# First attention of a two-layer encoder: where its next weights are requested and split, on which queue layer 1's memory stores go, and where the rest of layer 1's bias is laid out

## The chip, the cores and the metric

One core of a Trainium2 chip. The metric is the device time of one execution in microseconds. Before the change it is 2130.92 us, the median of three runs (2130.47 to 2131.5); one more execution was taken by the profiler, and the views below are of that one.

In the profile, PE is TensorE's matmul and PEld its weight load, DVE is VectorE, ACT ScalarE, POOL GpSimd; SPq and ACTq are the queues on which SyncE and ScalarE issue DMAs, each in order.

## The reference

An encoder of two layers on 1024 tokens of width 1024, with 256 fixed memory tokens. Each layer has a token mixer, a cross attention to the memory and a SwiGLU:

```python
mem_n = rmsnorm(mem, norm_mem)
for i in range(DEPTH):                       # DEPTH = 2
    h = rmsnorm(x, norm_mix[i])
    mkv = mem_n @ w_mem_kv[i]                # memory keys and values, 4 heads
    if i % 2 == 0:
        proj = h @ w_in_a[li]                # q (12 heads), k, v (4 heads), q_mem
        y_tok = windowed_gqa(...)            # window of +-128 tokens, ALiBi, sink
    else:
        proj = h @ w_in_b[li]                # q, k, v (12 heads each), q_mem
        y_tok = neighbourhood_attn(..., rpb_b[li])   # learned 2-D bias
    y_mem = memory_attn(qm, mk, mv)
    x = x + jnp.concatenate([y_tok, y_mem], axis=-1) @ w_out[i]
    h = rmsnorm(x, norm_ffn[i])
    gu = h @ w_gate_up[i]
    x = x + (jax.nn.silu(gu[..., :D_FF]) * gu[..., D_FF:]) @ w_down[i]
return rmsnorm(x, norm_final)
```

All of it is float32. The kernel reaches that precision by writing each operand of the dense products as a high part (rounded to fp32r by a cast, `hi`) and a low part (what the cast lost, `lo`, one subtraction), and by three matmuls for each product (`three`): high by high, high by low, low by high.

## The kernel before

Activations lie transposed, 128 features on the partitions and 512 tokens in a tile; the sequence is two halves of 512, f = 0 and 1. `steps` (L131 to L144) multiplies one unit of weights, 128 output features by 1024 inputs, with one half: eight steps of three matmuls of 128x128 by 128x512, so 24 matmuls for a unit and a half. The matmuls are recorded at L140, the splits at L106 (`hi`, ACT) and L109 (`lo`, DVE, or POOL where `load_w` is told so).

The program is written in Python and traced; a planner then lays the instructions out on each engine and each DMA queue. Its starting order is that of the program, but an instruction whose inputs its model finds ready can be put ahead of an earlier one that waits. On the chip each engine and each queue keeps the order that it was given. A tile with a tag has a fixed number of buffers (`bufs`); a new tile of that tag waits for the release of an old one.

**The opening (L325 to L345).** The first weights (`raws[0]`, in two halves) and the norm vectors (`gains`, L327) are loaded on ACT's queue; x, the memory, the memory's weights (`load_wm`) on SP's. `unscaled(k)` (L352) scales tile k of x's first half by the norm vector and splits it into `hT[0][k]`; the norm's factor itself is multiplied in later. Squares for the norms are recorded at L366. The first three units of layer 0 (`FIRST`: queries and keys of head group 0, memory queries, values) are multiplied with half 0 into three sums.

**The memory's units (the loop over i from 0 to 7).** Eight units of memory weights, four for each layer. Iteration i requests unit i+4 (`load_wm`), splits unit i+2 (`split_wm`) and multiplies unit i (`mem_dense`, L425). The other steps are threaded through it: the norm of half 1, the split of half 1 into `hT[1]` (`f1`), and `finish_wm(j)`, which turns the sums of unit j into memory keys (high and low) or values (transposed on TensorE, L448, then scaled and split, L453 and L454). When a layer's keys or values are complete, they are stored to DRAM: keys at L441 (`memk_d`), values at L458 (`memv_d`), both layers on SP's queue.

**The late sums.** After the loop, the same three units are multiplied with half 1 into `late`: the first two as a pair, step by step, with what is left of `finish_wm` between their steps; then the third. Their weights are the three buffers of the tag "whl" (`wf`).

**The attention of layer 0.** Twelve units in all: `Unit.request` asks for the raw weights on SP's queue (tile `w_early`, L587), `fetch` splits them, `open` makes the tiles, `half(f)` multiplies, `put` copies a sum into queries, keys or the transposed values, `close` copies the keys to the other 64 partitions (L647) or transposes the values (`put_v`, L564). `first_units` requests units 3 to 5, puts the six sums of the first three units, and closes them. Next, in program order, are sixteen DMAs (L871) that lay layer 1's bias out in DRAM; layer 1's attention reads it.

The attention itself runs over 32 halves of heads (`Half`): `scores` (L714, softmax on DVE, ACT and POOL), `turn` (transposes of the probabilities, L757) and `mix` (L777). Between their steps `pull()` draws one step of the remaining nine units (`other_units`), at a rate such that each unit is done when its head is due: the steps left over, divided by the halves left until then.

The lines ahead of the change that matter most here:

```python
pair_steps = zip(*(steps(late[n], wf[n], hT[1]) for n in range(2)), strict=True)
for i, _ in enumerate(pair_steps):
    if i > 0:
        run_some(todo, 1)
    if i == 1:
        run(todo)
        todo = (None for j in range(4, 8) for _ in finish_wm(j))
```

Of the kernel before, what the change touches and what calls it, by code (L numbers as in the profile page):

```python
# [41 lines left out]
def trunk_kernel(ctx: ExitStack, tc: tile.TileContext, a: dict, out: bass.AP):  # L42
# [103 lines left out]
    def run(g):  # L146
        for _ in g:
            pass

    def run_some(g, n):  # L150
        for _ in range(n):
            next(g, None)
# [134 lines left out]
    with tc.tile_pool(name="mp", bufs=1, reuse_waits="tile") as mp:  # L287
# [35 lines left out]
        raws = [raw_tile("wf_raw") for _ in range(3)]  # L323
        src = [a["w_in_a"][u] for u in FIRST[0]]
        nc.scalar.dma_start(raws[0][:, :HS], src[0][:, :HS])  # L325
        load_x(0, 0, each=True)
        nc.scalar.dma_start(gains, a["gains"])  # L327
        load_x(0, 2)
# [32 lines left out]
        def total(norm, parts, n=D):  # L361
# [14 lines left out]
            yield  # L376

        split_raw(wf[0], raws[0], cs=slice(0, HS))
        for k in range(4):
            unscaled(k)  # L380
# [49 lines left out]
        def finish_wm(i):  # L430
# [4 lines left out]
            if u < 2:  # L435
                nc.vector.tensor_tensor(t, ps, scale, op=ALU.mult)
                hi(kh[:, u], t)
                lo(kl[:, u], t, kh[:, u])
                if u == 1:
                    for j, h in enumerate((kh, kl)):  # L440
                        nc.sync.dma_start(memk_d[l, j], h.rearrange("p m k -> p (m k)").bitcast(F32))  # L441
                yield
                return
# [13 lines left out]
            if u == 3:  # L457
                nc.sync.dma_start(memv_d[l], vm.rearrange("p b m i d -> p (b m i d)").bitcast(F32))  # L458
            yield

        todo, f1 = iter(()), iter(())
        for i in range(8):
# [31 lines left out]
            if i > 4:  # L494
                run_some(f1, 2)
                run_some(todo, 2)
        run(f1)
        late = [ps_mm.tile([P, HS], F32, tag="mm", name="mm") for _ in range(2)]
        pair_steps = zip(*(steps(late[n], wf[n], hT[1]) for n in range(2)), strict=True)
        for i, _ in enumerate(pair_steps):  # L500
            if i > 0:
                run_some(todo, 1)
            if i == 1:
                run(todo)
                todo = (None for j in range(4, 8) for _ in finish_wm(j))
        run(todo)
        late.append(ps_t.tile([P, HS], F32, tag="T", name="mm"))
# [3 lines left out]
    for layer in range(2):  # L511
        is_a = layer == 0
        with tc.tile_pool(name=f"ap{layer}", bufs=1, reuse_waits="tile") as ap:
# [321 lines left out]
            def first_units():  # L835
                if is_a:
                    for z in units[n0 : 2 * n0]:
                        z.request()
                for z, (z.w, *ps) in zip(units, pre):
                    z.open()  # L840
                    z.put(0, ps[0])
                for n, z in enumerate(units[:n0]):
                    if is_a:
                        z.put(1, pre[n][2])
                    else:
                        yield from z.half(1)
                    units[n0 + n].fetch()
                    z.close()

# [17 lines left out]
            at = [0]  # L867
            run(first_units())
            if is_a:
                for r in range(ROWS):  # L870
                    nc.sync.dma_start(  # L871
                        bias_d[:, r * SC : (r + 1) * SC, :],
                        a["rpb"][:, :, (ROWS - 1 - r) * 24 : (ROWS - 1 - r) * 24 + 3 * P],
                    )
            work = other_units()
# [37 lines left out]

            run(halves[0].scores())
            groups = 13
            for i in range(len(halves)):
# [9 lines left out]
                if i == 0:  # L926
                    for _ in range(8):
                        pull()
                jobs = []
                if i + 1 < len(halves):  # L930
# [755 lines left out]
```

## Time and profile before

| what | value |
|---|---|
| median of three runs | 2130.92 us (2130.47 to 2131.5) |
| the profiled execution | 2130.05 us |
| its span, which all windows and times below count from | 2128.3 us |
| TensorE busy | 2096.2 us, 98% of the span |
| VectorE, ScalarE, GpSimd busy | 71%, 50%, 27% |
| mean granted TensorE clock | 0.996 of full speed |
| TensorE busy from 71.84 to 83.08 us | 8.12 of 11.24 us, granted clock 0.70 |
| TensorE busy from 90 to 320 us (most of the first attention) | 224.97 of 230 us, granted clock 1.00 |

How to read the rows. A row of waits names the engine, the line that waited, and whose end released it, then the total in us, the number of times and the longest. A row of the timeline has the start, the time, the engine and line, the operation, the tiles written and read, and in brackets the idle time just ahead of it and its releaser. A row of windows has the stretch, its length, the busy time of the engines asked for (instructions in brackets; PE, PEld, DVE, ACT, POOL where all are shown, PE alone where there is one), the granted clock, the share of the DMA engines and GB/s. A row of the chain has start, time and what the end waited for. Ends of matmuls are modelled, so single durations overlap; a rate is taken from the chain or from a long run of them.

### The profile page before, as it was taken

Reading aid. Unit: us, or ns where it says so; the run is one execution under the profiler, and the core shown is the slowest. Engines: PE = TensorE matmul, PEld = TensorE weight load, DVE = VectorE, ACT = ScalarE, POOL = GpSimd, SP = SyncE. Lnnn points to the kernel's source line nnn. Section 1 sums busy time; section 2 is a strip of 40 time slices with the busy share of each in tenths; the row PEclk is TensorE's granted clock in tenths of the full one; section 3 lists DMA queues with packets and bytes.
Section 4 is the critical chain, followed back from the end, with each engine's and each line's share of the span. In section 5 each row is a group of like instructions: output and inputs, shape, how many; then the busy total and the mean of one; then the engine's idle time right before and its main releaser. Section 6 shows DMA issues by size and latency. Waiting matters only on the chain.

```text
span 2128.3 us, 29044 instructions
## 1 busy us (share of the span) xinstructions
PE 2096.2 (98%) x10316; PEld 1751.5 (82%) x10316; DVE 1518.6 (71%) x2476; ACT 1066.0 (50%) x2035; POOL 580.9 (27%) x618
## 2 busy tenths in 40 slices
PE   9999999999999999999999999999999999999998
PEld 7788888878888888888778888888788888888886
DVE  7687787787666666867765666667986666667675
ACT  6677775444434334344465666654443434344442
POOL 0344330233444430000233233203243444400000
PEclk9999999999999999999999999999999999999999
DMA  5421028333323227856232222274232323267662
GB/s 221 141 95 51 26 90 282 99 99 114 109 102 107 99 104 252 311 209 213 75 92 84 72 58 71 83 257 158 71 113 104 109 105 106 97 251 253 204 221 90
DMA packets 120914, 287.29 MB, mean 135 GB/s; under 512 B 12224, under 2 KB 20672, under 8 KB 120768
## 3 DMA queue, kind: packets, MB, share of 16 engines
q1 hardware_dynamic: 113312, 272.68, 37.9%
q10 hardware_dynamic: 7456, 12.74, 1.6%
q8 instruction: 82, 1.34, 0.3%
q14 instruction: 64, 0.52, 0.1%
HBM read 210.40 MB, written 68.94 MB: 131 GB/s over the span
## 4 chain that ended last, share of the span: by engine, by line
PE 89%; DVE 4%; ACT 3%; DMA 1%; issue 1%; POOL 1%; SPq 0%; DVEq 0%; POOLq 0%; ACTq 0%
PE X L1051 16%; PE Y L1051 16%; PE mm L140 15%; PE X L1482 11%; PE Y L1482 8%; PE po L140 8%; PE O L777 3%; PE S L714 3%; PE pT L757 3%; PE X L1133 2%; PE Y L1133 2%; ACT p L729 1%; PE mm L425 1%; DMA wd_kept<-in_w_dn 1%; PE bc L249 0%
## 5 line engine op out<-in xcount | busy, mean ns | idle before, releaser
L1051 PE MATMUL Y<-hB,wgu 128*128 128x512 f32 x1056 | 255.5, 391 | 0.8 <-ACT c L1071 0.8
L1051 PE MATMUL X<-hB,wgu 128*128 128x512 f32 x1056 | 254.8, 391 | 0.0
L1482 PE MATMUL X<-hB,wd 128*128 128x512 f32 (+1 forms) x1092 | 243.7, 383 | 0.9 <-DVE x L1446 0.9
L109 DVE TENSOR_TENSOR wgu<-wS,wgu 128x1024 fp32r<-128x1024 f32 (+1 forms) x124 | 152.9, 1233 | 121.7 <-ACT wgu L106 121.5
L1482 PEld LDWEIGHTS X<-hB,wd 128*128 128x128 f32 x1092 | 200.2, 188 | 41.8 <-issue 2.3
L1051 PEld LDWEIGHTS Y<-hB,wgu 128*128 128x128 f32 x1056 | 196.7, 188 | 43.4 <-ACT c L1071 1.6
L1051 PEld LDWEIGHTS X<-hB,wgu 128*128 128x128 f32 x1056 | 195.9, 188 | 39.9
L742 POOL TENSOR_SCALAR p<-p,stat 128x384 f32<-128x384 f32 (+1 forms) x256 | 142.0, 574 | 308.8 <-DVE stat L739 214.4
L140 PE MATMUL mm<-hT,wqk 128*128 128x512 f32 x672 | 197.2, 405 | 1.5 <-DVE KL L109 1.5
L106 ACT CAST wgu<-wS 128x1024 fp32r<-128x1024 f32 (+1 forms) x124 | 114.3, 923 | 150.2 <-POOL wS L1008 124.6
L140 PE MATMUL po<-yT,wo 128*128 128x512 f32 x768 | 185.0, 394 | 0.0
L1482 PE MATMUL Y<-hB,wd 128*128 128x512 f32 x792 | 181.0, 390 | 0.1
L1482 PEld LDWEIGHTS Y<-hB,wd 128*128 128x128 f32 x792 | 148.4, 188 | 32.0 <-DVE x L1446 0.8
L234 POOL TENSOR_TENSOR nr<-nv,neg_half 128x4 f32<-128x4 f32 (+1 forms) x12 | 13.4, 1118 | 585.8 <-DVE nv L233 582.0
L140 PEld LDWEIGHTS po<-yT,wo 128*128 128x128 f32 x768 | 142.7, 188 | 29.6 <-issue 1.0
L1051 PE MATMUL X<-hT,wgu 128*128 128x512 f32 x624 | 150.2, 391 | 0.0
L106 ACT CAST hB<-b_raw 128x512 fp32r<-128x512 f32 x154 | 89.5, 618 | 116.8 <-DMA b_raw<-b_d 96.7
L1008 POOL TENSOR_TENSOR wS<-wgu_raw 128x512 f32<-128x512 f32 x44 | 61.1, 1388 | 294.5 <-DVE wgu L109 294.5
L1051 PEld LDWEIGHTS X<-hT,wgu 128*128 128x128 f32 x624 | 116.7, 188 | 26.3
L729 ACT ACTIVATE p<-p,stat 128x256 f32<-128x256 f32 (+1 forms) x192 | 112.4, 587 | 51.9 <-DVE stat L725 49.9
L109 DVE TENSOR_TENSOR pl<-pT,ph 128x384 fp32r<-128x384 f32 (+1 forms) x256 | 118.2, 492 | 19.9 <-ACT ph L106 16.9
L109 DVE TENSOR_TENSOR hB<-b_raw,hB 128x512 fp32r<-128x512 f32 x154 | 100.0, 687 | 43.3 <-ACT hB L106 42.8
(208 smaller groups left out, 4232.2 us busy)
## 6 DMA issues: line engine op xcount, KB each, us to landing
wgu_raw<-in_w_gu SPq DMA_DIRECT2D x92, 512.0 KB
wd_raw<-in_w_dn SPq DMA_DIRECT2D x70, 512.0 KB
b_raw<-b_d SPq DMA_DIRECT2D x70, 512.0 KB
b_d<-c SPq DMA_DIRECT2D x88, 256.0 KB
b_d<-t SPq DMA_DIRECT2D x66, 256.0 KB
wo_raw<-in_w_out SPq DMA_DIRECT2D x32, 512.0 KB
xr_d<-x ACTq DMA_DIRECT2D x32, 256.0 KB
xr<-xr_d SPq DMA_DIRECT2D x16, 512.0 KB
```

The lines of the kernel that those rows point to most:

```text
L106: nc.scalar.copy(dst, src)
L109: (eng or nc.vector).tensor_tensor(dst, src, h.bitcast(F32), op=ALU.subtract)
L140: nc.tensor.matmul(ps[:, :n], l, r, start=start and i == 0 and j == 0, stop=stop and i == len(order) - 1 and j == 2,)
L714: nc.tensor.matmul(s_[:, :n], Q[self.h][:, qb * P : (qb + 1) * P], k, start=j == 0, stop=j == 1)
L729: nc.scalar.activation(p[:, :n], p[:, :n], AF.Exp, bias=m1, scale=-1.0, accum_out=s1)
L742: nc.gpsimd.tensor_scalar(p[:, :n], p[:, :n], ri[:, i : i + 1], 1.0, op0=ALU.mult, op1=ALU.mult)
L757: nc.tensor.transpose(tr[:, j * P : (j + 1) * P], p[:, j * P : (j + 1) * P], ident)
L777: nc.tensor.matmul(o[:, c0 : c0 + w * P], self.value(j), t[:, s0 : s0 + w].rearrange("p j q -> p (j q)"), start=j == js[0] and t is self.p ...
L1008: sub = lambda o, p_, q_: nc.gpsimd.tensor_tensor(o, p_, q_, op=ALU.subtract)
L1051: nc.tensor.matmul(ps, l, r, start=n in (0, 1, 3, 6) and k == 0 and i == 0, stop=k == 3 and i == 2, skip_group_check=True,)
L1133: nc.tensor.matmul(bank[:, at : at + h2], l, r, start=start and k == 0 and i == 0, stop=stop and k == 1 and i == 2, skip_group_check=True,)
L1482: nc.tensor.matmul(bank[:, c], l, r, start=i in (0, 1, 3, 6) and p == 0 and n == 0, stop=p == HF - 1 and n == 2, skip_group_check=True,)
```

## The change

Five edits, all ahead of or inside the first attention.

1. The norm vectors are loaded ahead of the first weights on ACT's queue, and `unscaled(0)` stands ahead of the split of these weights.
2. The stores of layer 1's memory keys and values go on ACT's queue; layer 0's stay on SP's.
3. In iteration 5 of the memory's loop, unit 3's raw weights are requested on SP's queue (`next_raw`). The pair of late sums is taken apart: `late[0]` with all its steps, then `late[1]`; at the first step of `late[1]` unit 3's weights are split, on ACT and DVE, into the buffer that `late[0]`'s weights leave. The leftover steps of `finish_wm` stand at steps 5 to 7 of the one and from step 0 on of the other.
4. Layer 0's first units become `ready_units`: units 4 and 5 alone are requested there, and three steps are drawn (`pull`) ahead of the transposes of the values. One step is also drawn behind each of the four steps of the first scores.
5. The sixteen DMAs of layer 1's bias are issued two at a time in halves 4 to 11 of the attention.

```diff
--- before.py
+++ after.py
@@ -322,9 +322,9 @@
 
         raws = [raw_tile("wf_raw") for _ in range(3)]
         src = [a["w_in_a"][u] for u in FIRST[0]]
+        nc.scalar.dma_start(gains, a["gains"])
         nc.scalar.dma_start(raws[0][:, :HS], src[0][:, :HS])
         load_x(0, 0, each=True)
-        nc.scalar.dma_start(gains, a["gains"])
         load_x(0, 2)
         nc.scalar.dma_start(raws[0][:, HS:], src[0][:, HS:])
         load_x(0, 4)
@@ -375,8 +375,9 @@
             norm.acc = [t[:, :n]]
             yield
 
+        unscaled(0)
         split_raw(wf[0], raws[0], cs=slice(0, HS))
-        for k in range(4):
+        for k in range(1, 4):
             unscaled(k)
         split_raw(wf[0], raws[0], cs=slice(HS, D))
         for k in range(4, NK):
@@ -438,7 +439,7 @@
                 lo(kl[:, u], t, kh[:, u])
                 if u == 1:
                     for j, h in enumerate((kh, kl)):
-                        nc.sync.dma_start(memk_d[l, j], h.rearrange("p m k -> p (m k)").bitcast(F32))
+                        queues[l].dma_start(memk_d[l, j], h.rearrange("p m k -> p (m k)").bitcast(F32))
                 yield
                 return
             nc.scalar.copy(t, ps)
@@ -455,10 +456,11 @@
                     vl, src[:, b], r, vh.bitcast(F32), op0=ALU.mult, op1=ALU.subtract
                 )
             if u == 3:
-                nc.sync.dma_start(memv_d[l], vm.rearrange("p b m i d -> p (b m i d)").bitcast(F32))
+                queues[l].dma_start(memv_d[l], vm.rearrange("p b m i d -> p (b m i d)").bitcast(F32))
             yield
 
-        todo, f1 = iter(()), iter(())
+        queues = nc.sync, nc.scalar
+        todo, f1, next_raw = iter(()), iter(()), []
         for i in range(8):
             if i % 4 == 0:
                 l = i // 4
@@ -494,15 +496,22 @@
             if i > 4:
                 run_some(f1, 2)
                 run_some(todo, 2)
+            if i == 5:
+                next_raw = raw_tile("wf_raw")
+                nc.sync.dma_start(next_raw, a["w_in_a"][1])
         run(f1)
         late = [ps_mm.tile([P, HS], F32, tag="mm", name="mm") for _ in range(2)]
-        pair_steps = zip(*(steps(late[n], wf[n], hT[1]) for n in range(2)), strict=True)
-        for i, _ in enumerate(pair_steps):
-            if i > 0:
-                run_some(todo, 1)
+        for i, _ in enumerate(steps(late[0], wf[0], hT[1])):
             if i == 1:
                 run(todo)
                 todo = (None for j in range(4, 8) for _ in finish_wm(j))
+            if i > 4:
+                run_some(todo, 1)
+        next_w = wp.tile([P, 2, D], F32R, tag="whl", name="wf", bufs=3)
+        for i, _ in enumerate(steps(late[1], wf[1], hT[1])):
+            run_some(todo, 1)
+            if i == 0:
+                split_raw(next_w, next_raw)
         run(todo)
         late.append(ps_t.tile([P, HS], F32, tag="T", name="mm"))
         run(steps(late[2], wf[2], hT[1]))
@@ -833,18 +842,27 @@
             n0 = 3
 
             def first_units():
-                if is_a:
-                    for z in units[n0 : 2 * n0]:
-                        z.request()
+                for z, (z.w, ps) in zip(units, pre):
+                    z.open()
+                    z.put(0, ps)
+                for n, z in enumerate(units[:n0]):
+                    yield from z.half(1)
+                    units[n0 + n].fetch()
+                    z.close()
+
+            def ready_units():
+                units[n0].w = next_w
+                for z in units[n0 + 1 : 2 * n0]:
+                    z.request()
                 for z, (z.w, *ps) in zip(units, pre):
                     z.open()
                     z.put(0, ps[0])
                 for n, z in enumerate(units[:n0]):
-                    if is_a:
-                        z.put(1, pre[n][2])
-                    else:
-                        yield from z.half(1)
+                    z.put(1, pre[n][2])
                     units[n0 + n].fetch()
+                    if z.kind == "v":
+                        for _ in range(3):
+                            pull()
                     z.close()
 
             def other_units():
@@ -865,13 +883,15 @@
 
             done = [n0]
             at = [0]
-            run(first_units())
-            if is_a:
-                for r in range(ROWS):
-                    nc.sync.dma_start(
-                        bias_d[:, r * SC : (r + 1) * SC, :],
-                        a["rpb"][:, :, (ROWS - 1 - r) * 24 : (ROWS - 1 - r) * 24 + 3 * P],
-                    )
+            if not is_a:
+                run(first_units())
+
+            def spread_bias(r):
+                nc.sync.dma_start(
+                    bias_d[:, r * SC : (r + 1) * SC, :],
+                    a["rpb"][:, :, (ROWS - 1 - r) * 24 : (ROWS - 1 - r) * 24 + 3 * P],
+                )
+
             work = other_units()
             taken = [0]
 
@@ -911,7 +931,11 @@
                 for m in range(2):
                     yield from steps(po[m], wo[m], yT[0], pairs[-2:-1], start=False, stop=False)
 
-            run(halves[0].scores())
+            if is_a:
+                ready_units()
+            for _ in halves[0].scores():
+                if is_a:
+                    pull()
             groups = 13
             for i in range(len(halves)):
 
@@ -926,6 +950,9 @@
                 if i == 0:
                     for _ in range(8):
                         pull()
+                if is_a and 4 <= i < 4 + ROWS // 2:
+                    for r in (2 * i - 8, 2 * i - 7):
+                        spread_bias(r)
                 jobs = []
                 if i + 1 < len(halves):
                     jobs.append(halves[i + 1].scores())
```

## The prediction

> **What bounds the kernel now.** The page's table of engines and its chain come first, then the waits of the matrix engine over the whole span.
>
> ```profile
> PE 2096.2 (98%) x10316; PEld 1751.5 (82%) x10316; DVE 1518.6 (71%) x2476; ACT 1066.0 (50%) x2035; POOL 580.9 (27%) x618
> PE 89%; DVE 4%; ACT 3%; DMA 1%; issue 1%; POOL 1%; SPq 0%; DVEq 0%; POOLq 0%; ACTq 0%
> ...
> PE mm L140 <- ACT hT L355: 2.5, 1, 2.5
> PE mm L140 <- ACT wqq L106: 2.4, 1, 2.4
> ```
>
> TensorE is the bound, so only its waits can be gained. The two rows of waits are single events inside the part that the diff edits: the opening (ACT hT, 2.5 us) and the first weights of layer 0's attention (ACT wqq, 2.4 us). The timeline of TensorE and the windows by stage show the second.
>
> ```profile
> 70.78 1.07 PE L140 MATMUL mm<-hT,wf 128*128 128x512 f32 x4
> 72.53 1.09 PE L564 MATMUL vtr<-ident,vT 128*128 128x128 f32 x8 [0.68 <-ACT vT L607]
> 76.07 7.01 PE L140 MATMUL mm<-hT,wqq 128*128 128x512 f32 x17 [2.45 <-ACT wqq L106]
> 82.92 0.40 PE L714 MATMUL S<-mKH,QS 128*128 128x256 f32 x2
> ...
> 58.13 4.15 PE mm L140 x18
> 52.46 0.22 PE mvT L448 x2
> ...
> 75.40:75.60 0.20, 0.00 (x0) 0.52 0.90 369
> ...
> 82.20:82.40 0.20, 0.20 (x2) 0.92 0.65 223
> ```
>
> The last product with the first three weights ends at 70.78 + 1.07 = 71.85. Then eight transposes stand alone, then 2.45 us of nothing, then 17 matmuls in 7.01 us, though 18 took 4.15 us at 58.13 (0.231 each). The windows say why: the granted clock is at half (0.52) from 75.4 and back (0.92) at 82.2. The chain of waits and SP's timeline say why the weights were late.
>
> ```profile
> 69.72 5.22 DMA w_early<-in_w_in_a
> ...
> SPq L441 <- ACT mkh L106: 19.3, 2, 18.4
> SPq L458 <- DVE mv L454: 4.4, 1, 4.4
> ...
> 67.98 0.33 SPq L458 DMA_DIRECT2D memv_d<-mv  x1
> 68.36 0.76 SPq L871 DMA_DIRECT2D bias_d<-in_rpb  x1
> 69.72 1.40 SPq L587 DMA_DIRECT2D w_early<-in_w_in_a  x3
> ```
>
> SP's queue is in order. It stood 4.4 us on the store of layer 1's memory values (memv_d, 67.98); behind it came a piece of layer 1's bias (and dist), and only at 69.72 the weights, which took 5.22 us to land, while TensorE needed them at 71.85.
>
> **The change part by part.** *The stall.* From 71.85 to the first score at 82.92 (11.07 us) TensorE did 17 matmuls (17 x 0.231 = 3.92 us) and eight transposes (8 x 0.11 = 0.88, by the mvT row): 4.80 us of work, so **6.27 us lost** (0.68 + 2.45 of waits, the rest half clock and slow transposes). Making unit 3's weights ready beforehand and queueing three steps of its product ahead of the transposes takes this away, if nothing else is late at 71.85.
>
> *What is late next: the weights.*
>
> ```profile
> 56.30 0.34 SPq L441 DMA_DIRECT2D memk_d<-mkh  x1
> 54.55 3.36 PE L140 MATMUL mm<-hT,wf 128*128 128x512 f32 x14
> 74.97 1.04 ACT L106 CAST wqq<-w_early 128x1024 fp32r<-128x1024 f32 x1 [1.40 <-DMA w_early<-in_w_in_a]
> 19.64 1.22 DVE L109 TENSOR_TENSOR wm<-wm 128x1024 fp32r<-128x1024 f32 x1
> 60.00:70.00 10.00, 10.00 (x47) 8.19 (x47) 5.21 (x13) 5.08 (x13) 0.00 (x0) 1.00 0.46 169
> ```
>
> next_raw is requested in iteration 5, ahead in program order of both layers' memory stores. If it is put behind layer 0's keys store (issued at 56.30, where SP stood 18.4 us), it lands by 56.9 + 5.2 = 62.1, by the slow w_early row. Its split (next_w) takes wf[0]'s buffer, so it must wait for the end of late[0]: 54.55 + 24 x 0.231 + 0.2 = 60.3.
>
> The split is one cast of 1.04 on ACT and one subtraction of 1.22 on DVE: ready by about 65, seven early. Both engines are half idle from 60 to 70 (DVE 5.21, ACT 5.08 of 10 us), so it costs nothing; without that cover it would be the 2.3 us. Units 4 and 5 still come by w_early, but are needed only after 48 matmuls (11 us) more.
>
> *What is late next: the bank.* Unit 3's sum takes the bank that late[0] leaves, so the puts (the copies of late[0] into queries and keys) must be done.
>
> ```profile
> 67.20 0.37 ACT L453 ACTIVATE mv<-mvT,nr 128x128 fp32r<-128x128 f32 x1 [0.42 <-DVE mv L454]
> 67.47 0.61 ACT L106 CAST QS<-first 64x512 fp32r<-64x512 f32 x1
> ...
> 73.11 0.70 DVE L109 TENSOR_TENSOR KL<-mm,KH 64x512 fp32r<-64x512 f32 x1 [0.64 <-ACT KH L106]
> 59.52 0.68 DVE L109 TENSOR_TENSOR hT<-h,hT 128x512 fp32r<-128x512 f32 x1
> ```
>
> Today the last read of it ends at 73.81, which would cost 73.81 - 71.85 = 1.96 us. What held the puts until 67.47 is the last memory value (mv, 67.20), whose transposes stand in TensorE's order after all eight steps of the pair (48 matmuls). Now the six leftover steps stand at steps 5 to 7 of late[0] and 0 to 2 of late[1], so that transpose comes after some 33: 15 x 0.231 = 3.5 us earlier. Against that ACT gains 1.04 for next_w and three stores to issue. Net some 1.3 us earlier, and late[0] itself ends 5 us earlier, so its keys need not go behind vT. Bounds 0 to 1.96; I take 0.1, near the lower end, as three of the four movements are in its favour.
>
> *late[0] alone.* One weight per step asks for a new hT every 3 x 0.231 = 0.69 us, where the pair asked every 1.4. The last hT is ready at 60.20 (DVE, 59.52); late[0]'s eighth step would want it near 59.6. Bounds: nothing (late[1]'s first steps go into the hole) to 0.6; I take 0.3.
>
> *The stores on ACT's queue.* Three issues, and waits behind DVE:
>
> ```profile
> 1.23 0.39 ACTq L327 DMA_DIRECT2D gains<-in_gains  x1
> 61.85 0.43 DVE L109 TENSOR_TENSOR mkl<-mt,mkh 128x256 fp32r<-128x256 f32 x1 [0.15 <-ACT mkh L106]
> 66.42 0.37 ACT L453 ACTIVATE mv<-mvT,nr 128x128 fp32r<-128x128 f32 x1 [2.73 <-PE mvT L448]
> ```
>
> An issue takes 0.39 us (gains); the low keys that a store waits for take 0.43 on DVE. Queued behind each on ACT are next_w's cast, the last mv and the puts, for which TensorE waits in the end. Three times 0.4 to 0.8 us is 1.2 to 2.4; ACT stands idle 2.73 us ahead of mv at 66.42, so the cost is taken as zero; without that cover up to 2.4 on the puts, which the bank's bound holds mostly.
>
> *The opening.* gains first, and unscaled(0) ahead of the split.
>
> ```profile
> 4.39 0.62 ACT L106 CAST wf<-wf_raw 128x512 fp32r<-128x512 f32 x1 [1.62 <-DMA wf_raw<-in_w_in_a]
> 5.20 1.06 ACT L366 ACTIVATE sq<-x 128x1024 f32<-128x1024 f32 x1 [0.20 <-DMA x<-in_x]
> 8.17 1.33 ACT L355 ACTIVATE hT<-x,gains 128x512 fp32r<-128x512 f32 x2 [0.69 <-DMA x<-in_x]
> 8.93 1.42 DVE L356 SCALAR_TENSOR_TENSOR hT<-x,gains,hT 128x512 fp32r<-128x512 f32 x2 [0.61 <-ACT hT L355]
> 10.00:20.00 10.00, 10.00 (x44) 8.09 (x43) 10.00 (x15) 10.00 (x16) 0.00 (x0) 1.00 1.04 403
> ```
>
> A square (1.06) is ahead of the first hT on ACT. With hT first, TensorE starts up to 1.06 earlier, less 0.39 for weights that now queue behind gains: 0.7. But at 8.17 ACT waits for x's second transfer, and from 8.93 DVE has no gap (10.00 of 10.00 in the next window), so what TensorE wins before 8 it waits away after. Bounds: -0.4 (the weights' delay shown) to +0.7; I take 0.
>
> *Bias pieces and pulls.* Sixteen pieces leave SP's queue here and come in halves 4 to 11. Seven more pulls (four among the first scores, three at the values unit) move matmuls forward and add none. Both at zero; what they cost uncovered stands among the rivals.
>
> **Sum:** 6.27 - 0.1 - 0.3 = 5.9 off the profiled run of 2130.05 (span 2128.3): 2124.2. The median of the runs shown is 0.87 higher, 2130.92, so **2125.0**.
>
> **The clock rule.**
>
> ```profile
> 6.90:7.50 0.60, 0.57 (x1) 1.00 0.91 331
> ```
>
> In the trace the clock halved some 3.5 us after the last matmul (71.85 to 75.4), with transposes in between, and was full again or still (1.00 at 6.90) behind the 2.5 us ahead of the first product. [...]
>
> **The rivals.**
> 1. *A wait at the joint in place of the old one.* Bank 1.96 and hT 0.6 both fall due: gain 6.27 - 2.56 = 3.7, time 2127.2. For it: the puts end at 73.81 today. Against: their last cause moves 3.5 us forward.
> 2. *Given back in the attention.*
>
> ```profile
> 90.00:320.00 230.00, 224.97 (x1285) 189.18 (x1285) 182.83 (x484) 177.16 (x479) 92.21 (x159) 1.00 0.19 61
> ```
>
> If the softmax chain over DVE and ACT sets the halves' time, the seven pulls taken from later halves (7 x 3 x 0.231 = 4.8 us) leave holes there: gain 5.9 - 4.8 = 1.1, time 2129.8. Against: TensorE is busy 224.97 of 230, DVE 182.83, ACT 177.16.
> 3. *It doesn't do what it says.* The order in the queues is a planner's; if next_raw or w_early is still put behind the stores, nothing moves: 2130.9.
> 4. *Slower.* The sixteen pieces in halves 4 to 11 stand in SP's queue ahead of key copies and weights.
>
> ```profile
> L871 SPq DMA_DIRECT2D bias_d<-in_rpb x16: 737/748/922, 34.5 to 85.1; - x16
> SPq L647 <- ACT KH L106: 33.0, 2, 24.4
> ```
>
> At 0.75 each, 12.0 us of queue. It decides where a key copy lands after the score that reads it; on the path in full, 5.9 - 12.0 is 6.1 slower: 2137.0. Against: SP itself waited 33.0 us for keys to copy, so it has room.
> 5. *More.* Half of the attention's 5.03 us of idleness goes too, as the first head's keys come some 8 us earlier, and the opening's 0.7 stays: 2125.0 - 2.5 - 0.7 = 2121.8.
>
> **How the numbers follow.** Forecast (2123 to 2126.6): 0.53. Joint 0.14, given back 0.13, not done 0.04, slower 0.06, more 0.10. 0.2%, about what a measurement of this kernel can tell from no change, is 4.26 us: faster means below 2126.66. Forecast and "more" are faster (0.63), and a third of the joint's cases: 0.67. The rest of the joint, given back and not done: 0.27. Slower 0.06. The range reaches from just under "more" to given back, 2121.0 to 2130.0, leaving out the slower case, not done, and tails.
>
> **What would show it.** Right: no row of waits "mm <- ACT wqq" near 72, the clock at 1.00 throughout, next_w's subtraction on DVE near 62 to 65, stores of layer 1 on ACTq, w_early on SP before 66, the first score near 75. Opening right: a first product earlier than now, with DVE still full from 10 to 20. Wrong: a wait for KL or QS at the joint (rival 1), an attention that starts earlier but ends no earlier (rival 2), scores waiting on KH copies (rival 4).

## The result, and the profile after

| | before | after |
|---|---|---|
| median of 18 runs each, same chip | 2129.95 us (2127.08 to 2131.5) | 2125.82 us (2123.74 to 2127.43) |
| span of the profiled execution | 2128.3 us | 2124.1 us |
| mean granted clock | 0.996 | 0.998 |

The ratio is 0.998, with a 95% interval of 0.9973 to 0.9987: faster by 4.1 us, where 5.9 were forecast. The time lies 0.8 us above the forecast one. It is closer than the gain by luck: over 18 runs the median of before came out 0.97 us lower than the 2130.92 that the forecast started from, and that hides more than half of the 1.8 us by which the gain is short.

First the waits of TensorE over the whole span, after the change (engine, line, whose end released it; total, times, longest).

```profile
PE mm L140 <- DVE KL L109: 2.7, 3, 1.5
PE mm L140 <- ACT wf L106: 2.4, 1, 2.4
PE vtr L573 <- ACT vT L616: 1.6, 1, 1.6
```

The 2.4 us on wqq is gone; the 2.4 on wf is the opening's, ahead of the first product. The wait for vT (the copy of the third late sum) has grown from 0.68 to 1.57. At the joint (where the late sums end and the attention begins) a wait of 0.57 for KL (the low keys of the first late sum) is new; the other two of that row lie behind the first attention, and before has them too. TensorE's timeline of the changed kernel shows where they lie.

```profile
66.40 6.17 PE L140 MATMUL mm<-hT,wf 128*128 128x512 f32 x26
74.14 0.77 PE L573 MATMUL vtr<-ident,vT 128*128 128x128 f32 x5 [1.57 <-ACT vT L616]
75.47 2.35 PE L140 MATMUL mm<-hT,wf 128*128 128x512 f32 x9 [0.57 <-DVE KL L109]
...
77.91 0.37 PE L723 MATMUL S<-mKH,QS 128*128 128x256 f32 x1
```

The late sums end at 66.40 + 6.17 = 72.57; then 1.57 us of waiting, five transposes, 0.57 us of waiting, and unit 3's matmuls with weights that have long been there. So 2.14 us of waiting stand where 3.13 stood. The first score comes at 77.91 instead of 82.92. The clock doesn't drop:

```profile
73.00:74.00 1.00, 0.00 (x0) 1.00 0.60 193
75.00:76.00 1.00, 0.53 (x2) 1.00 0.78 232
```

These are two windows of TensorE (length, busy time, clock, DMA share, GB/s). Next, the timelines of ACT, DVE and the queues in the changed kernel: how the weights came early, and what came late in their place.

```profile
38.30 0.33 SPq L501 DMA_DIRECT2D wf_raw<-in_w_in_a  x1
62.84 3.71 SPq L596 DMA_DIRECT2D w_early<-in_w_in_a  x2
...
62.02 1.05 ACT L106 CAST wf<-wf_raw 128x1024 fp32r<-128x1024 f32 x1 [1.40 <-PE mm L140]
63.10 1.22 DVE L109 TENSOR_TENSOR wf<-wf_raw,wf 128x1024 fp32r<-128x1024 f32 x1 [1.70 <-ACT wf L106]
...
66.19 1.25 ACTq L442 DMA_DIRECT2D memk_d<-mkl  x1
...
69.42 0.62 ACT L106 CAST QS<-first 64x512 fp32r<-64x512 f32 x1 [0.79 <-DVE mv L455]
...
73.52 0.57 ACT L616 COPY vT<-mm 128x512 f32<-128x512 f32 x1
74.11 0.58 ACT L106 CAST KH<-mm 64x512 fp32r<-64x512 f32 x1
...
74.72 0.69 DVE L109 TENSOR_TENSOR KL<-mm,KH 64x512 fp32r<-64x512 f32 x1
```

The planner put the request even ahead of layer 0's stores (from 56.9), at 38.30; the split was done at 64.3, eight early. But the puts began at 69.42, not earlier than the 67.47 of before, and ended at 75.41 (KL), 1.6 us later than the 73.81 of before. In ACT's order the copy of vT (73.52) still stands ahead of the cast of the keys (74.11).

**A ledger.** From the start of the late sums to the first matmul of the feed-forward (PE X on the chain) the matrix engine has the same 1779 instructions, transposes included, in both kernels, so opening and feed-forward stay out. Windows of all engines: stretch, length, then busy time of PE, PEld, DVE, ACT and POOL with instructions in brackets, clock. First before, then after; of each the whole length, and the attention alone.

```profile
54.55:400.34 345.79, 337.43 (x1779) 280.13 (x1778) 261.43 (x601) 236.15 (x578) 116.69 (x185) 0.99 0.36 118
84.00:320.00 236.00, 230.77 (x1315) 193.33 (x1313) 186.60 (x493) 181.09 (x493) 94.25 (x163) 1.00 0.20 65
```

```profile
55.16:396.69 341.53, 335.15 (x1779) 277.63 (x1778) 263.81 (x602) 236.72 (x578) 112.47 (x181) 1.00 0.36 118
84.00:320.00 236.00, 232.02 (x1319) 194.19 (x1318) 186.13 (x489) 179.77 (x486) 91.00 (x161) 1.00 0.20 64
```

The length falls by 345.79 - 341.53 = 4.26 us. Busy time falls by 337.43 - 335.15 = 2.28 (the half clock). Idle time is 8.36 before, of it 5.23 in the attention (236.00 - 230.77) and 3.13 at the joint; after, 6.38, of it 3.98 in the attention and 2.40 at the joint. So 4.26 = 2.28 of clock + 0.73 at the joint + 1.25 in the attention. The forecast had some 3.1 + 3.1 + 0 from these three, less 0.4. Most of what is missing is the joint's waits, where only 0.73 of 3.1 was gained; the busy time fell by 0.8 less than forecast.

### The profile page after: what moved, and what is told of

Its sections match the earlier page's. It is cut to its first block, busy times and chain, and to the rows that moved or that the text cites. A ratio compares the mean times of both kernels' runs of the same rounds, so it can differ in the third digit from the quotient of the medians.

```text
span 2124.1 us, 29029 instructions
## 1 busy us (share of the span) xinstructions
PE 2094.9 (99%) x10316; PEld 1749.5 (82%) x10316; DVE 1521.0 (72%) x2477; ACT 1066.8 (50%) x2035; POOL 576.0 (27%) x614
## 3 DMA queue, kind: packets, MB, share of 16 engines
q8 instruction: 82, 1.34, 0.3%
## 4 chain that ended last, share of the span: by engine, by line
PE 90%; DVE 4%; ACT 2%; issue 1%; DMA 1%; POOL 1%; ACTq 0%; DVEq 0%; SPq 0%; POOLq 0%
PE X L1078 16%; PE Y L1078 16%; PE mm L140 15%; PE X L1509 11%; PE Y L1509 8%; PE po L140 8%; PE O L786 3%; PE S L723 3%; PE pT L766 3%; PE X L1160 2%; PE Y L1160 2%; PE mm L426 1%; DMA wd_kept<-in_w_dn 1%; DVE pl L109 0%; PE bc L249 0%
```

## The experiments

The time of the whole run can't tell tenths: from the feed-forward on all of them are the same program, and in the fourteen profiles this rest took 1726.8 to 1729.9 us. So the length of the ledger is the main measure, with its idle part (length less busy).

| kernel | length, us | PE idle in it | wait at the joint | median, us | ratio to before, 95% |
|---|---|---|---|---|---|
| before | 345.79 | 8.36 | 3.13 | 2129.95 | |
| before, second profile | 343.75 | 7.28 | 2.15 | 2129.01 (one run) | |
| e10, opening alone | 345.86 | 8.65 | 3.51 | 2130.46 | 1.0002 (0.9993 to 1.0011) |
| after | 341.53 | 6.38 | 2.14 | 2125.82 | 0.998 (0.9973 to 0.9987) |
| e5, after again | 340.90 | 5.66 | 1.31 | 2125.48 | 0.9982 (0.9972 to 0.9991) |
| e1, opening undone | 340.51 | 5.44 | 1.30 | 2126.71 | 0.998 (0.9971 to 0.9989) |
| e2, stores on SP | 340.37 | 5.06 | 1.25 | 2125.65 | 0.9979 (0.997 to 0.9988) |
| e3, first square early | 340.78 | 5.56 | 1.34 | 2126.29 | 0.9981 (0.9971 to 0.999) |
| e8, and no pulls | 340.95 | 6.39 | 0.98 | 2126.01 | 0.9982 (0.9973 to 0.9991) |
| e6, bank and square | 338.55 | 4.13 | 0 | 2122.96 | 0.9972 (0.9961 to 0.9984) |
| e11, bank | 338.29 | 3.81 | 0 | 2124.19 | 0.997 (0.9958 to 0.9982) |
| e12, bank, opening undone | 338.28 | 3.81 | 0 | 2123.42 | 0.9966 (0.9954 to 0.9979) |

Each kernel was timed against before on its own chip (2129.82 to 2130.52 there).

### The change repeated: is 2.14 us the wait's size?

No edit.

> The changed kernel once more, beside the others on one chip. In its first profile the joint's waits were 1.57 + 0.57, in three kernels with the same late sums 0.73 + 0.57, and the only row that differs ahead of them is the issue of the low keys' store on ACT (1.25 us against 0.36 to 0.38). Theory: that was a chance of one execution; here the issue takes 0.4 us, the joint's waits are 0.7 + 0.6, and the feed-forward starts near 395.8 instead of 396.7. Rival: it belongs to this kernel's order; then 1.25 and 2.1 again.

TensorE's timeline of this second profile of the changed kernel:

```profile
73.05 0.77 PE L573 MATMUL vtr<-ident,vT 128*128 128x128 f32 x5 [0.74 <-ACT vT L616]
```

And from ACT's:

```profile
65.91 0.36 ACTq L442 DMA_DIRECT2D memk_d<-mkl  x1
```

The wait for vT is 0.74 here, and 0.57 for KL again: 1.31 us. In the first profile the issue of memk_d<-mkl held ACT for 1.25 us (the row above); here it took 0.36, and 0.36 to 0.38 in the six other profiles with this store on ACT's queue. ACT was late by that. So 1.3 is the joint's usual wait, and the other 0.8 a chance of one execution.

### The stores back on SP's queue

```diff
-        queues = nc.sync, nc.scalar
+        queues = nc.sync, nc.sync
```

> The changed kernel with layer 1's memory stores back on SP's queue. Theory: on ACT's queue the store of the low keys (issued 66.19, 1.25 us) and that of the values (waits for DVE until 69.06) hold the last memory values and the puts behind them; the first put (QS<-first) starts at 69.42, 1.95 us later than before. Undone: first put near 67.6, last read of late[0] near 73.5, unit 3's first matmul near 73.6 instead of 75.47, waits at the joint 0.3 instead of 2.1 us, time some 1.8 us below the changed kernel, about 2124.0. Rival: the puts are late because of the cast of unit 3's weights and TensorE's order; then the first put moves by under 0.8 us, and w_early and the memory keys' loads, which now stand behind the stores on SP, cost it again: time 2125.5 to 2127.

ACT's timeline, then TensorE's, of this kernel:

```profile
67.36 0.61 ACT L106 CAST QS<-first 64x512 fp32r<-64x512 f32 x1
...
72.27 0.58 ACT L616 COPY vT<-mm 128x512 f32<-128x512 f32 x1 [0.73 <-PE mm L140]
72.88 0.58 ACT L106 CAST KH<-mm 64x512 fp32r<-64x512 f32 x1
...
72.91 0.76 PE L573 MATMUL vtr<-ident,vT 128*128 128x128 f32 x5 [0.68 <-ACT vT L616]
```

My theory was that the stores on ACT cause the wait. It fell. Without them the puts do begin earlier (67.36, against 68.07 with the opening undone, e1, whose late sums start 0.18 us before e2's), but then ACT stands 0.73 us ahead of vT, for the end of the third late sum, and the keys' cast stands behind vT in ACT's order. The wait is the same 1.25. The stores cost ACT 0.7 to 0.9 us that TensorE doesn't miss, as long as their issues are short: the zero of the forecast holds, by a cover it didn't name. Only in the first profile, with its issue of 1.25 us, did they cost the joint 0.8.

### Another bank for unit 3's first sum

```diff
-                    ps = bank.tile([P, HS], F32, tag="T", name="mm") if bank else mm_tile()
+                    ps = bank.tile([P, HS], F32, tag="O" if bank is ps_o else "T", name="mm") if bank else mm_tile()
...
-                        yield from z.half(f)
+                        yield from z.half(f, ps_o if is_a and n == n0 and f == 0 else None)
```

The first run of it has the early square of e3 too; e11 has the change's opening, e12 the opening of before.

> Experiment e3 (square early), with unit 3's first sum in the bank that the norms and mix use, which is free at the joint, instead of the one that late[0] leaves. Theory: the 1.3 us that are left at the joint in e1 to e3 are the wait for that bank, whose last reader (KL) stands on ACT and DVE behind the copy of the last late sum (vT), on whatever queue the stores go; with a free bank unit 3 follows the late sums without a gap, waits at the joint 0 to 0.2 us, first matmul of unit 3 near 72.0, feed-forward's start 1.2 us earlier than in e3 (395.2), near 394.0. Rival: something else is late there (unit 3's weights or the transposes' input), and a wait of 0.7 to 1.3 stays.

> The changed kernel with one edit: unit 3's half 0 is summed in a bank of ps_o, so that it doesn't wait for the queries' and keys' copies of late[0]; the opening is the change's. Theory: no wait at the joint, 1.3 to 2.1 us off the change's feed-forward start (396.69, 395.79), so 394 to 395; time 1.3 to 2 us under the change, 2123.5 to 2124.5, ratio to before 0.9970 to 0.9978. Rival (the lower time of the earlier kernel with this bank came from its opening): feed-forward start 395 to 396.5, time as the change.

> The kernel just above with before's opening in place of the change's. Theory (the change's opening costs 0.3 to 0.6 us): feed-forward start 393.5 to 394.5, 0.3 to 0.6 us below the one just above, time lower by as much, which the intervals can't part. Rival (the opening is worth nothing either way): the same start within 0.2 us of it when the late sums start at the same time.

The timeline of TensorE in e11, and its ledger:

```profile
66.44 10.50 PE L140 MATMUL mm<-hT,wf 128*128 128x512 f32 x45
76.78 1.04 PE L573 MATMUL vtr<-ident,vT 128*128 128x128 f32 x8
77.57 2.53 PE L140 MATMUL mm<-hT,wf 128*128 128x512 f32 x10
```

```profile
55.21:393.50 338.29, 334.48 (x1779) 277.54 (x1778) 263.88 (x602) 236.26 (x578) 112.25 (x181) 1.00 0.36 119
```

Forty-five matmuls in one piece from 66.44, no wait, and the transposes in the middle of work. So the bank was what TensorE waited for: with nothing else changed the length goes from 341.53 and 340.90 to 338.29. That is 2.6 to 3.2 us for a wait of 1.31 to 2.14. The rest: busy time is 0.67 lower (335.15 to 334.48), and idle time outside the joint is lower by 0.4 to 0.5 (6.38 - 2.14 = 4.24 and 5.66 - 1.31 = 4.35, against 3.81). That the gap cost busy time here as well is what the rows show; which instructions take it was not followed. All three kernels are faster than before by 5.6 to 6.9 us in their medians, and 7.2 to 7.5 by length (first profile of before). Against the change they gain 2.3 to 3.3 us of length (338.3 to 338.6 against 340.9 and 341.5), more than the 1.3 to 2.1 expected of e11; the intervals of their ratios overlap the change's.

### The opening: undone, alone, and with the first square early

e1 is the changed kernel with before's opening:

```diff
-        nc.scalar.dma_start(gains, a["gains"])
         nc.scalar.dma_start(raws[0][:, :HS], src[0][:, :HS])
         load_x(0, 0, each=True)
+        nc.scalar.dma_start(gains, a["gains"])
...
-        unscaled(0)
         split_raw(wf[0], raws[0], cs=slice(0, HS))
-        for k in range(1, 4):
+        for k in range(4):
```

> The changed kernel with the opening of the kernel before (first weights ahead of the norm vectors, unscaled(0) behind the split). Theory: in the changed kernel the first square has moved behind the scaled tiles on ACT and stands ahead of the second weights' cast; that made the second product start at 15.39 instead of 14.79, and everything up to the joint 0.6 us late. Undone: second product at 14.8, first norm sums (st) at 23.3, late sums' start at 54.6, time 0.6 us below the changed kernel, about 2125.2. Rival: the 0.6 us comes from DMA landings that differ from run to run; then st stays near 23.9 and the time near 2125.8.

e10 is the kernel before with the change's two lines alone.

> The kernel before with the first edit alone: gains requested first, and unscaled(0) ahead of the first split. Theory (the planner puts the first square behind, ahead of wf[1]'s cast, and the subtraction waits): late sums start 0.3 to 0.6 us later than in before (54.55), square near 12.1, time 0 to 0.6 us above before, ratio 1.000 to 1.0003. Rival (only the phase of the clock differs between executions): square still near 5.2 or late sums start within 0.1 of 54.55. As forecast: no change in time. The joint is that of before.

e3 is the changed kernel with the first square right behind `unscaled(1)`:

```diff
-        for k in range(1, 4):
+        unscaled(1)
+        parts = total(norms[0], [xp[k, 0] for k in range(0, NK, 2)])
+        run_some(parts, 1)
+        for k in range(2, 4):
```

> The changed kernel, with the first square of the norm written right behind unscaled(1), so that it falls into ACT's wait for x's second transfer. Theory: then the new opening costs nothing: second weights' cast near 12.1, second product near 14.5, st near 23.0, late sums' start near 54.3, time 0.6 to 0.9 us below the changed kernel, about 2125.0. Rival (the order on ACT doesn't matter, DVE does): second product stays near 15.4 and the time near 2125.8.

What the edit does is plain. Timelines of ACT and DVE in the changed kernel:

```profile
12.10 1.05 ACT L366 ACTIVATE sq<-x 128x1024 f32<-128x1024 f32 x1
13.05 1.03 ACT L106 CAST wf<-wf_raw 128x1024 fp32r<-128x1024 f32 x1
...
14.11 1.23 DVE L109 TENSOR_TENSOR wf<-wf_raw,wf 128x1024 fp32r<-128x1024 f32 x1 [0.80 <-ACT wf L106]
```

The square left its place at 5.20, ahead of the first product, and went to 12.10, ahead of the cast of the second weights; DVE waits 0.80 for that cast. In e10 TensorE's timeline shows the hole that follows:

```profile
6.82 8.52 PE L140 MATMUL mm<-hT,wf 128*128 128x512 f32 x26 [2.43 <-ACT wf L106]
15.86 8.69 PE L140 MATMUL mm<-hT,wf 128*128 128x512 f32 x37 [0.53 <-DVE wf L109]
```

The first product begins earlier (6.44 to 6.82 in the five profiles with this opening, against 6.90 to 7.01), and in three of the five the second begins late (waits of 0.53, 0.33 and 0.17 us in e10, e2 and e5). The sum of both is small, and the executions scatter more than it. The eight norm matmuls behind the three products (st, L213) start at 23.91, 23.56, 23.64, 24.40 and 23.97 with the change's opening (after, e2, e5, e10, e11; mean 23.90) and at 23.31, 23.37, 23.17, 24.20, 24.28 and 23.64 with before's (before, e1, e4, e7, e9, e12; mean 23.66). A quarter of a us, with 0.3 to 0.5 of scatter: not told from zero, and e10's ratio of 1.0002 says no more. The early square gives 22.93, 23.53 and 22.98 (e3, e6, e8; mean 23.15), half a us below either; but two of these three executions, e3 and e8, had the shortest slow starts of all fourteen (see the last section), so that this isn't shown to be the edit's, and its medians don't tell it apart.

### The pulls taken out

This is e3 without the seven steps drawn ahead.

```diff
-                    if z.kind == "v":
-                        for _ in range(3):
-                            pull()
...
-            for _ in halves[0].scores():
-                if is_a:
-                    pull()
+            run(halves[0].scores())
```

> Experiment e3 without the seven steps drawn ahead (three at the values unit, four among the first scores). Theory: the planner puts unit 3's matmuls behind the late sums anyway as soon as their weights and bank are ready, so the pulls are worth only the order around the values' transposes: joint's waits up by 0 to 0.5 us, feed-forward's start within 0.5 us of e3 (395.2). Rival: the pulls carry part of the gain; feed-forward's start 1 us or more later than in e3.

```profile
73.72 0.97 PE L140 MATMUL mm<-hT,wf 128*128 128x512 f32 x3 [0.24 <-DVE KL L109]
74.59 0.47 PE L725 MATMUL S<-mKH,QS 128*128 128x256 f32 x2
...
78.74 0.38 PE L725 MATMUL S<-mKH,QS 128*128 128x256 f32 x1 [0.91 <-ACT p L732]
```

In TensorE's timeline of this kernel the first score comes at 74.59, 1.5 us before e3's 76.14, and then TensorE waits 0.91 for the softmax (ACT p). The length is 340.95 against e3's 340.78: the seven pulls are worth nothing that one profile each can tell.

### The half clock of before: matmuls or transposes in the gap

In the kernel before, unread work behind the eight transposes: two float32 products of vT (recorded as four matmuls; e4), or sixteen transposes (e7). e9 is the kernel before, unchanged.

```diff
+                    if is_a and z.kind == "v":
+                        keep = ps_o.tile([P, HS], F32, tag="O", name="keep")
+                        for _ in range(2):
+                            nc.tensor.matmul(keep, ones, z.vt[:, HS:], start=True, stop=True)
```

and, in place of the last two lines,

```diff
+                        for c in range(16):
+                            nc.tensor.transpose(keep[:, c % 4 * P : (c % 4 + 1) * P], z.vt[:, c % 8 * P : (c % 8 + 1) * P], ident)
```

> The kernel before, with two extra matmuls of 128x512 float32 on the transposed values of the third unit, whose sums nobody reads, behind the values' transposes, where TensorE waits for unit 3's weights. The weights are as late as before. Theory: of the 6.27 us lost at the joint some 3 are the half clock, which an idle stretch without matmuls causes; with the extra matmuls the clock stays at 1.00 from 75 to 83, unit 3's first 14 matmuls take some 3.3 us, and the time falls by 3 us against the kernel before, about 2127.0. Rival (the transposes count as work and the wait itself sets the clock back, or the loss lies in the weights' low part from POOL): clock 0.5 again, or no gain: 2130.

> The kernel before, with sixteen extra transposes of 128x128 in the place of e4's two extra matmuls (sums that nobody reads). TensorE is then busy with transposes for some 3 us of the 3.5 us behind the last matmul. Theory (transposes do not hold the clock up): the granted clock falls to 0.50 near 75.4 all the same, and the first score is near 83, as before; time as before, 2130.5. Rival (any work of TensorE holds the clock): 1.00 throughout, first score near 80.4, as in e4, time 2129 to 2129.6.

> The kernel before, unchanged, for a second profile of its joint. Theory: the half clock from 75.4 us is a regular part of the stall, because eight transposes (1.09 us) between two stretches without matmuls don't hold the clock: the 17 matmuls behind the wait for wqq take about 7.0 us again, first score near 82.9 us, feed-forward from 400.3. [...]

TensorE's timelines: e4, then e7, then the second profile of before, and of the last two windows of all engines (the clock stands behind the five engines).

```profile
73.33 1.88 PE L852 MATMUL keep<-vT,ones 128*128 128x512 f32 x4
76.35 3.84 PE L140 MATMUL mm<-hT,wqq 128*128 128x512 f32 x14 [1.14 <-ACT wqq L106]
```

```profile
74.35 1.91 PE L852 MATMUL keep<-ident,vT 128*128 128x128 f32 x16
76.59 3.84 PE L140 MATMUL mm<-hT,wqq 128*128 128x512 f32 x14 [0.33 <-ACT wqq L106]
```

```profile
73.50 1.09 PE L564 MATMUL vtr<-ident,vT 128*128 128x128 f32 x8 [0.68 <-ACT vT L607]
76.06 6.15 PE L140 MATMUL mm<-hT,wqq 128*128 128x512 f32 x17 [1.47 <-ACT wqq L106]
82.06 0.40 PE L714 MATMUL S<-mKH,QS 128*128 128x256 f32 x2
```

```profile
77.00:78.00 1.00, 1.00 (x4) 0.82 (x5) 0.00 (x0) 0.56 (x1) 1.00 (x2) 0.75 1.09 232
80.00:81.00 1.00, 1.00 (x4) 0.81 (x3) 0.76 (x2) 0.79 (x4) 1.00 (x3) 0.55 1.13 227
```

The half clock belongs to the stall: it is there in all three profiles of a kernel with before's joint (before, e9, e10), and absent in e4 and e7, where the gap was filled (1.00 in every window of 1 us from 71 to 84 in both). Its size and that of the wait vary, though. By the clock records of the traces it lasted 6.83 us in before (from 75.41) and in e10 (from 76.41), and 3.41 us in e9 (from 77.49). In e9 the weights landed 4.3 us after their issue (70.71 to 74.97), not 5.2, so the wait was 1.47. By the working of the forecast (first score, less the end of the late sums, less 4.80 of work) the stall there is 82.06 - 72.82 - 4.80 = 4.44 us, and in e10 84.18 - 72.94 - 4.80 = 6.44: the 6.27 was one draw of 4.4 to 6.4. Filling the gap didn't make before faster, where 3 us were expected of e4 (lengths 345.04 and 344.28, ratios 0.9996, 0.9987 to 1.0005, and 1.0003, 0.9994 to 1.0012): the weights were as late as ever, and TensorE's idle time from 84 to 320 us rose to 6.26 (e4) and 6.52 (e7) from 5.23.

## Why the prediction was right, and where it was off

**The stall and the weights: right.** No run takes edit 3 out. That it carries the gain is read from the trace, and from what the others are worth: e10, e2 and e8 find nothing for the opening, the stores and the pulls. Edit 5 wasn't tried alone. Request at 38.30, split at 63.10 to 64.3 (forecast: near 62 to 65), no wait for wqq, w_early at 62.84 (before 66), layer 1's stores on ACTq, clock at 1.00. The first score, forecast near 75, came at 77.91. The forecast's stall is gone in full in e11, where 345.79 - 338.29 = 7.50: 6.27 and 1.42 from the attention (5.23 - 3.81) are 7.69.

**The bank: mis-sized, and this is the miss.** "Bounds 0 to 1.96; I take 0.1, near the lower end" measured 1.25 to 1.34 us in four of the six profiles with this bank, 0.98 in e8 and 2.14 in the first; with all that hangs on it, 2.6 to 3.2, more than the upper bound. Two reasons given for the low end were false.

- "that transpose comes after some 33: 15 x 0.231 = 3.5 us earlier". TensorE's timelines, before and then e1 (whose late sums start at the same 54.6), with a row of DVE's in e1 at the end:

```profile
54.55 3.36 PE L140 MATMUL mm<-hT,wf 128*128 128x512 f32 x14
57.88 4.39 PE L140 MATMUL mm<-hT,wf 128*128 128x512 f32 x18
62.25 3.90 PE L140 MATMUL mm<-hT,wf 128*128 128x512 f32 x16
66.00 0.38 PE L448 MATMUL mvT<-ident,mt 128*128 128x128 f32 x2
```

```profile
54.62 3.36 PE L140 MATMUL mm<-hT,wf 128*128 128x512 f32 x14
57.96 5.30 PE L140 MATMUL mm<-hT,wf 128*128 128x512 f32 x22
63.35 2.53 PE L140 MATMUL mm<-hT,wf 128*128 128x512 f32 x10
65.71 0.38 PE L448 MATMUL mvT<-ident,mt 128*128 128x128 f32 x2
...
73.37 0.69 DVE L109 TENSOR_TENSOR KL<-mm,KH 64x512 fp32r<-64x512 f32 x1 [0.28 <-ACT KH L106]
```

  14 + 22 + 10 = 46 matmuls stand ahead of it, not 33 (48 in before), and it comes 0.3 us earlier. The Python loops offer a step there; the order on the engine is the planner's.
- "its keys need not go behind vT". They still do: vT at 72.27 and KH at 72.88 in e2, in that order on ACT even where ACT stood idle ahead of both. So, in that order, the keys' bank can't be free before the third late sum ends, plus a copy, a cast and a subtraction. In e1 that is 72.05 to 74.06 (KL, 73.37 + 0.69), 2.0 us, of which the five transposes cover 0.77.

**late[0] alone: 0.1 instead of 0.3.** No wait on hT shows, and the late sums take 72.57 - 55.16 = 17.4 us where they took 71.85 - 54.55 = 17.3.

**Stores on ACT at zero: right**, as e2 shows; the cover was ACT's wait for the third late sum, not the idle 2.73 us named.

**The opening at zero: within what can be told**, as the eleven profiles show. "A first product earlier than now" came true (6.75); "DVE still full from 10 to 20" did not, as it stood 0.80 ahead of 14.11. The square is the step that the working left out: whatever jumps ahead pushes something into another place.

**Bias pieces and pulls at zero: not contradicted, the pieces hardly tested.** No score waits for a key copy; e8 answers the pulls. The planner put twelve of the sixteen pieces back to between 35 and 85 us on SP's queue, where all of them were before; four went to 116 to 123.

**The rivals.** The joint wait came true in its bank half: 1.3 to 2.1 of the 1.96. The sign that the forecast named for it, a wait for KL at the joint, is there, and the measured gain of 4.1 lies nearer this rival's 3.7 than the 5.9 of the forecast. Its sum takes the waits at their own length, with no half clock behind them; the windows of the changed kernel bear that out (1.00, with 2.14 us of waiting). "Given back in the attention" was wrong in sign: idle time there fell by 1.25 us (5.04 to 5.23 in the three profiles with before's joint, 3.73 to 4.13 in the eight of the change with its pulls), so a part of "more" came true, and it paid for most of what the joint kept. Why the attention idles less was not tried; e8 has 4.50 (236.00 - 231.50 busy) without the pulls, so half a us of it hangs on them. "Slower" and "doesn't do what it says" did not happen.

So the forecast gain of 5.9 against the measured 4.1 comes out as: bank and what hangs on it -2.6 to -3.2 instead of -0.1, attention +1.25, and a stall that is 0.7 smaller in the mean of before's three lengths (345.13) than in the profile from which it was worked out (345.79). Together that makes 3.4 to 4.0, and the interval of the ratio allows 2.8 to 5.8.

## What to carry to other kernels

When a wait on weights goes, list the buffers that the work moved forward will write, and read from the trace of before when the last reader of each is done: here the bank's lateness stood there to the tenth (73.81 - 71.85 = 1.96 us, and 2.0 in e1), and a free bank elsewhere was worth another 2.6 to 3.2 us of length. Don't discount such a bound by where the source puts a step, as long as a planner orders the engines. Where edits are worth 1 us in 2100, compare the lengths of a stretch with equal work between two marks: here they lie within 0.3 us in the three kernels with the free bank and 0.6 in the two profiles of the change, but only within 2.1 in the three with before's joint, whose stall itself varies; the rest of the run scatters by 3.

## What the runs showed that was not expected

The first product runs at half speed for a time that changes from run to run, though the clock column says 1.00 there: a matmul starts every 0.43 us at first and every 0.23 later. Windows of the same two us, in before, then in e7, whose opening is the same (stretch, length, TensorE busy and its matmuls in brackets):

```profile
10.00:12.00 2.00, 2.00 (x9) 1.62 (x8) 2.00 (x4) 2.00 (x5) 0.00 (x0) 1.00 1.04 426
```

```profile
10.00:12.00 2.00, 2.00 (x6) 1.61 (x5) 2.00 (x4) 2.00 (x4) 0.00 (x0) 1.00 1.05 418
```

Nine matmuls against six, in an engine busy throughout. The step to 0.23 comes where the trace's clock record begins, at 10.55 in before and 12.62 in e7, and from 9.44 (e8) to 12.86 us (e11) in all; ahead of it the column has no record. Among the six profiles with before's opening this is nearly all the scatter: st goes from 23.17, where the step comes first (10.36, e4), to 24.28, where it comes last (12.64, e9). So the forecast's remark that the clock "was full again or still (1.00 at 6.90)" is not borne out: the column reads 1.00 where matmuls take twice their time. Why the number of slow first matmuls varies by run was not shown. What the traces show is that the clock falls 64.85 or 64.86 us after the first step in before, e9 and e10, though their late sums end at 71.84, 72.82 and 72.94, and it stays at half for 3.41 us or twice that; 64.85 is some nineteen times 3.41. So the 3.5 us that the forecast saw between the last matmul and the half clock is no fixed delay: in e9 it is 4.67 us (72.82 to 77.49), with matmuls running again from 76.06.

In e7 transposes seem to have held the clock. The stretch without matmuls (72.74, the end of the late sums, to 76.59) is 3.85 us long there, longer than e9's 3.24 (72.82 to 76.06), and filled with 24 transposes; the clock stays at 1.00, and the 14 matmuls behind it took 3.84 us, where e9's 17 took 6.15, with the clock at half for 3.41 us of them (the windows from 78 to 80 us hold six matmuls in each us in e7, four in e9). So the half clock near 75.4 that was expected of e7 did not come, and its first score, at 80.53, is that of the rival (80.4). The time of the first step doesn't part the two: it comes at 12.62 in e7 and at 12.64 in e9. But each is one execution, so this is seen once and not settled; the eight transposes alone (1.09 us) held the clock in none of the three profiles with before's joint.
